# Decoder trunk on one core: input and first weights fetched in halves of the features, first four output tiles accumulated by halves of the contraction, products of ones ahead of the input

## The chip, the cores and the metric

The kernel runs on one core of a Trainium2 chip. The metric is the device time of one execution in microseconds (us), the median of several runs. The core has a matrix engine (TensorE, PE in the profile; its weight loads are PEld), a vector engine (VectorE, DVE), an activation engine (ScalarE, ACT), a general engine (GpSimd, POOL), and queues from which transfers between main memory and the on-chip memory are issued (SyncE's is SPq, ScalarE's is ACTq). Products accumulate in PSUM tiles, which TensorE writes and VectorE or ScalarE read.

## The reference, cut to what matters

Two layers, each a SwiGLU feed-forward half-step, a token-mixing sub-layer, and a second feed-forward half-step, over 16 learned tokens and 256 input tokens of 1024 features. The change touches the entry and the first half-step:

```
h = jnp.concatenate([meta, x], axis=1)          # 16 + 256 tokens, 1024 features
for l in range(DEPTH):                          # DEPTH = 2
    h = h + 0.5 * swiglu(rms_norm(h, ffn1_norm[l]), ffn1_w_gu[l], ffn1_w_down[l])
    ...                                         # token mixing, second half-step
return rms_norm(h, final_norm)[:, N_META:]

def swiglu(x, w_gu, w_down):
    gate, up = jnp.split(x @ w_gu, 2, axis=-1)  # each 2816 columns
    return (jax.nn.silu(gate) * up) @ w_down
```

## The kernel before

All activations lie feature-major: eight tiles `h[k]` of 128 features by 272 tokens (`L`). Every wide product is made three times, from parts that add up to the exact operand: weight high part times activation high part, weight high times activation low, weight low times activation high (`mm3`, lines 163 to 165). For that, each piece of weights (128 partitions by 1024 values) is rounded by ScalarE into a high part `wh` (line 144), and VectorE subtracts to get the low part `wl` (line 145); both have four buffers. The raw weights come in units of 1 MB (8 contraction steps by 256 columns) into `raw`, which has three buffers. The input rows `xr` also lie in one of these three.

At the start, x is loaded as two transfers of 128 tokens by 1024 features (lines 194 and 198), the learned tokens `mr` as two small ones (line 197), the small vectors `rows` as one (line 193, on ScalarE's queue). The first two weight units (gate and up of the first 256 columns) come as four transfers of 512 KB, one for each piece of 128 columns and all eight contraction steps (line 135); later units as one transfer each (line 132). For each `k` in 0 to 7, TensorE transposes 16 + 128 + 128 tokens into one PSUM tile (lines 916 to 918); `norm.split` scales by the gain and splits (ScalarE line 249, VectorE line 250); the tile is copied to `h[k]` (lines 923 and 925). Then `norm.square` squares each `h[k]` on ScalarE and adds it to `acc` on VectorE (lines 259 to 263). One product of ones with `acc` (line 273, in `rstd`) sums the squares over the features, and a chain on VectorE and ScalarE (lines 275 to 289) makes the token factor, which `finish` (lines 313 to 320) applies to finished gate and up tiles.

`ffn_up` takes two pairs of tiles (gate in a PSUM tile of tag `mm`, up in one of tag `aux`, four buffers of each tag) per step `f2`. For `f2 == 0` it takes the gate tiles first (pieces 0 and 1), then the up tiles (pieces 2 and 3): four output tiles by eight contraction steps by three products, 96 products. `piece()` prepares weights two pieces ahead.

The order of instructions on each engine is not the order of the program text alone. The Tile framework puts every engine's instructions in an order before the run, by priority and by the times that it computes, and an instruction that is ready early may be put ahead of others; `tc.issue_after(i)` forces instructions of the same engine behind `i` (`early` does that for the first two pieces). On the chip each engine then runs its list in order. `consts` loads the tables `cst` and makes the lower bounds of the forget gates; the program calls it at `f2 == 1`.

Of the kernel before, what the change touches and what calls it, by code (L numbers as in the profile page):

```python
# [52 lines left out]
def trunk(ctx: ExitStack, tc: tile.TileContext, a: dict):  # L53
# [13 lines left out]
    V, S, E, GP = nc.vector, nc.scalar, nc.tensor, nc.gpsimd  # L67

# [8 lines left out]

# [1 line left out]
    units, plan, ready, early = [], [], [], {}  # L79
    AHEAD = 2  # L80
# [44 lines left out]
    raws = {}  # L125

    def prepare(u, k0, kn, c0, cn):
        src, kt, cols, per, cuts = units[u]
        if u not in raws:
            raws[u] = T([P, 2048], F32, "raw", 3)[:, :kt * cols].rearrange("p (k c) -> p k c", k=kt)  # L130
            if u > 1:
                nc.sync.dma_start(out=raws[u], in_=src)
        rw = raws[u][:, k0:k0 + kn, c0:c0 + cn]
        if u < 2:
            nc.sync.dma_start(out=rw, in_=src[:, k0:k0 + kn, c0:c0 + cn])
        w2 = [T([P, 1024], F32R, t, 4)[:, :kn * cn].rearrange("p (k c) -> p k c", k=kn) for t in ("wh", "wl")]
# [6 lines left out]
        for x, hw, lw in views or [(rw, *w2)]:  # L143
            S.copy(out=hw, in_=x)  # L144
            V.tensor_tensor(out=lw, in0=x, in1=hw.bitcast(F32), op=ALU.subtract)  # L145
        return [tuple(w[:, k] for w in w2) for k in range(kn)]

    used = [0]

    # the next piece, as a list over its contraction steps  # L150
    def piece():
        used[0] += 1
        while len(ready) < min(used[0] + AHEAD, len(plan)):
            with ExitStack() as st:
                for i in early.pop(len(ready), ()):
                    st.enter_context(tc.issue_after(i.ins))
                ready.append(prepare(*plan[len(ready)]))
        r, ready[used[0] - 1] = ready[used[0] - 1], None
        return r
# [10 lines left out]

# [6 lines left out]
    parts, o = [], 0  # L177
    for n in (L, L, P, H, 32, NBLK * 32, P):
        parts.append(cst[:, o:o + n])
        o += n  # L180
    cos_t, sin_t, causal, bdmask, eye32, lv, rowsel = parts
    lvmask = lv.bitcast(I32).rearrange("p (n c) -> p n c", c=32)
# [6 lines left out]

# [11 lines left out]
    ps = PS("aux")  # L201
    E.transpose(out=ps[:, 0:76], in_=rows, identity=ident[0:76, 0:76])
    V.tensor_copy(out=cols, in_=ps[:, 0:76])
    F1, MX, F2, FN, QN, KVN, HGN, LB = 0, 16, 32, 48, 56, 62, 66, 68
# [3 lines left out]

    # lower bounds of the forget gates, by a softmax over the layers
    lbt = T([P, 8, G], F32, "lbt")  # L210
# [17 lines left out]
    qns = T([P, 6], F32, "qns")  # L228
    V.tensor_scalar(out=qns, in0=cols[:, QN:QN + 6], scalar1=DQK ** -0.5, scalar2=None, op0=ALU.mult)

    def lbc(l, g):
        return lbt[:, 4 + l, g:g + 1], lbt[:, 6 + l, g:g + 1]

# [1 line left out]
    class Norm:  # L235
# [10 lines left out]
        def split(self, k, src):  # L246
# [5 lines left out]
            self.parts[k] = (xh, xl)  # L252
            return i, j

        def square(self, k):
# [24 lines left out]

    # in steps, so that other work can stand between them
    def rsqrt(out, m, c):
# [13 lines left out]

    # two or more output tiles; the last contraction step of all of them comes last
    def mm_group(items, n):
# [5 lines left out]

# [1 line left out]
    def ffn_up(norm, c):  # L306
# [15 lines left out]
        def item(ps):  # L322
            w = piece()
            return ps[:, c], lambda k: w[k], lambda k: norm.x(k, c)

        for f2 in range(NF // 2):
            pairs = [(PS("mm"), PS("aux")) for j in range(2)]
            for j in range(2):
                mm_group([item(pairs[i][j]) for i in range(2)] if f2 == 0 else [item(ps) for ps in pairs[j]], KD)
                if f2 or j:  # L330
# [6 lines left out]
            if f2 == 1 and start:  # L337
                start.pop()()
        return acts
# [14 lines left out]

    # the last one, token-major, with the norm of the output
    def ffn_out(norm, c):
# [40 lines left out]

# [1 line left out]
    def mix(l, norm, nxt):  # L399
# [30 lines left out]

        # latent queries, latent keys and values (each with its norm), the shared rotary key
        def latents():
# [42 lines left out]
        def heads():  # L475
            kpe = st["kpe"]
            # queries
            wq = piece() + piece() + piece()
# [23 lines left out]
            yield  # L502
            # keys and values
            wkv = piece() + piece()
# [38 lines left out]

        # recurrence inputs
        lo = NM if last else 0
# [65 lines left out]

        # attention
        oa = []
# [81 lines left out]

        # recurrence, by halving
        am = T([P, 256], F32, "am", 1)
# [3 lines left out]
        def halving(gr):  # L701
# [3 lines left out]

            # products inside blocks of 32 tokens
            def blocks(li):
# [22 lines left out]

            # products between the halves of blocks of 2 b tokens
            def halves(b):
# [16 lines left out]
            for li, b in enumerate(LEVELS):  # L749
# [77 lines left out]

        # the wide products are dealt out among the steps of the two mixers
        def chain(*gens):
# [11 lines left out]

        # a branch's projection, times its gate
        mg = []
# [64 lines left out]

# [1 line left out]
    ca = slice(0, L)  # L910
    cs = slice(NM, L)
    norm = Norm(F1, ca)
    for k in range(KD):
        ps = PS("mm" if k < 4 else "aux")
        ks = slice(k * P, (k + 1) * P)
        E.transpose(out=ps[:, 0:NM], in_=mr[k // 4][0:NM, k % 4 * P:(k % 4 + 1) * P], identity=ident[0:NM, 0:NM])
        E.transpose(out=ps[:, 16:144], in_=xr[:, 0, ks], identity=ident)
        E.transpose(out=ps[:, 144:272], in_=xr[:, 1, ks], identity=ident)
        after = norm.split(k, ps[:, ca])
        if k in (1, 3):  # L920
            early[len(early)] = after
        if k % 2:
            S.copy(out=h[k], in_=ps[:, ca])
        else:
            V.tensor_copy(out=h[k], in_=ps[:, ca])
# [66 lines left out]
```

## Time and profile before

| | |
|---|---|
| device time, three runs | 1232.86, 1233.23, 1233.68 us; median 1233.23 |
| span of the profiled execution, first to last instruction | 1232.4 us |
| so outside the span, against the median | about 0.8 us |
| TensorE busy | 1216.2 us, 99% of the span |
| VectorE busy, ScalarE busy, GpSimd busy | 870.1, 643.7, 8.6 us |
| read from main memory | 200.89 MB, 164 GB/s over the span |

The profile is of one execution. Its page gives the busy time of each engine and the chain of work that ended last: followed back from the last instruction, at each step to what released it, or to the instruction before it on its engine. The trace behind it can be asked for a stretch of time. Times within the trace are microseconds from the start of the span. Matmuls are pipelined: the duration of one in a row overlaps the next, so that the distance between the starts of two, or the chain's entry, is what one costs.

### The profile page before, as it was taken

The numbers are of one execution on the slowest core, as the hardware profiler recorded it, in microseconds if no ns is written. First come the engines' busy times: TensorE is split into PE (matmuls) and PEld (weight loads), VectorE is DVE, ScalarE is ACT, GpSimd is POOL, SyncE is SP. The second block draws the span as 40 slices with busy tenths as digits, with TensorE's granted clock in tenths as the row PEclk, the third lists the DMA queues.
The fourth block names the chain that finished last, engine by engine and source line by source line (L and its number), as shares of the span: only waits on it lengthen the run. The fifth ranks groups of instructions, "written<-read, shape, count | busy, mean of one in ns | idle before, by whom it ended". The sixth has DMA issues, their size and how long they took to land.

```text
span 1232.4 us, 24345 instructions
## 1 busy us (share of the span) xinstructions
PE 1216.2 (99%) x10210; PEld 1175.0 (95%) x10210; DVE 870.1 (71%) x1585; ACT 643.7 (52%) x1073; POOL 8.6 (1%) x28
## 2 busy tenths in 40 slices
PE   7999999999999999999999999999999999999997
PEld 6999999999988999999999999999998899999986
DVE  5877755787866877776558776558869586977743
ACT  5544444566774644444445444445776655545442
POOL 0000000000000000000000000000000000000000
PEclk9999999999999999999999999999999999999999
DMA  7645555545332545646555546555454345555651
GB/s 225 204 149 196 177 179 178 173 142 158 122 134 86 189 141 168 201 148 211 163 165 174 183 160 197 187 156 173 140 168 138 120 138 172 191 172 186 206 188 52
DMA packets 188781, 203.50 MB, mean 165 GB/s; under 512 B 3348, under 2 KB 176480, under 8 KB 188672
## 3 DMA queue, kind: packets, MB, share of 16 engines
q1 hardware_dynamic: 188272, 201.36, 50.4%
q8 instruction: 80, 1.31, 0.4%
q10 hardware_dynamic: 400, 0.60, 0.1%
q14 instruction: 29, 0.24, 0.1%
HBM read 200.89 MB, written 1.05 MB: 164 GB/s over the span
## 4 chain that ended last, share of the span: by engine, by line
PE 96%; ACT 2%; DVE 1%; DMA 1%; issue 0%; SPq 0%; POOLq 0%; POOL 0%
PE pmm L163 21%; PE pmm L164 21%; PE pmm L165 21%; PE paux L164 7%; PE paux L165 7%; PE paux L163 7%; PE pmm L373 2%; PE pmm L374 2%; PE pmm L375 2%; PE paux L643 1%; PE paux L714 1%; PE paux L688 1%; DMA raw<-x 1%; ACT wh L144 0%; ACT act L501 0%; PE paux L800 0%
## 5 line engine op out<-in xcount | busy, mean ns | idle before, releaser
L144 ACT CAST wh<-raw 128x1024 fp32r<-128x1024 f32 (+3 forms) x398 | 398.4, 1006 | 388.7 <-PE pmm L164 263.0
L145 DVE TENSOR_TENSOR wl<-raw,wh 128x1024 fp32r<-128x1024 f32 (+3 forms) x398 | 464.4, 1170 | 172.5 <-ACT wh L144 170.7
L163 PE MATMUL pmm<-x,wh 128*128 128x272 f32 (+1 forms) x1312 | 381.1, 291 | 0.7 <-ACT act L513 0.7
L165 PE MATMUL pmm<-x,wl 128*128 128x272 f32 (+1 forms) x1312 | 375.8, 287 | 0.0
L164 PE MATMUL pmm<-x,wh 128*128 128x272 f32 (+1 forms) x1312 | 375.6, 286 | 0.0
L163 PEld LDWEIGHTS pmm<-x,wh 128*128 128x128 f32 x1312 | 246.8, 188 | 3.0 <-ACT act L513 1.0
L164 PEld LDWEIGHTS pmm<-x,wh 128*128 128x128 f32 x1312 | 247.0, 188 | 0.9
L165 PEld LDWEIGHTS pmm<-x,wl 128*128 128x128 f32 x1312 | 246.4, 188 | 0.2
L163 PE MATMUL pmm<-act,wh 128*128 128x272 f32 (+1 forms) x836 | 239.8, 287 | 0.0
L164 PE MATMUL pmm<-act,wh 128*128 128x272 f32 (+1 forms) x836 | 239.1, 286 | 0.0
L165 PE MATMUL pmm<-act,wl 128*128 128x272 f32 (+1 forms) x836 | 238.9, 287 | 0.0
L163 PE MATMUL paux<-x,wh 128*128 128x272 f32 (+1 forms) x704 | 201.1, 286 | 0.0
L164 PE MATMUL paux<-x,wh 128*128 128x272 f32 (+1 forms) x704 | 201.1, 286 | 0.0
L165 PE MATMUL paux<-x,wl 128*128 128x272 f32 (+1 forms) x704 | 201.1, 286 | 0.0
L163 PEld LDWEIGHTS pmm<-act,wh 128*128 128x128 f32 x836 | 157.3, 188 | 1.0 <-issue 0.8
L164 PEld LDWEIGHTS pmm<-act,wh 128*128 128x128 f32 x836 | 157.5, 188 | 0.4 <-issue 0.4
L165 PEld LDWEIGHTS pmm<-act,wl 128*128 128x128 f32 x836 | 157.0, 188 | 0.5 <-issue 0.3
L163 PEld LDWEIGHTS paux<-x,wh 128*128 128x128 f32 x704 | 132.8, 189 | 0.0
L164 PEld LDWEIGHTS paux<-x,wh 128*128 128x128 f32 x704 | 132.6, 188 | 0.0
L165 PEld LDWEIGHTS paux<-x,wl 128*128 128x128 f32 x704 | 132.5, 188 | 0.0
L168 ACT CAST act<-tmp 128x272 fp32r<-128x272 f32 (+1 forms) x88 | 36.5, 415 | 124.4 <-DVE tmp L317 124.4
L313 DVE TENSOR_TENSOR tmp<-pmm,rstd 128x272 f32<-128x272 f32 (+1 forms) x88 | 38.3, 435 | 50.9 <-PE pmm L165 50.6
(239 smaller groups left out, 1058.9 us busy)
## 6 DMA issues: line engine op xcount, KB each, us to landing
raw<-ffn_w_gu SPq DMA_DIRECT2D x86, 1024.0 KB, 5.3
raw<-w_in SPq DMA_DIRECT2D x36, 1024.0 KB, 5.2
raw<-ffn_w_down SPq DMA_DIRECT2D x34, 1024.0 KB, 5.2
raw<-ffn_w_down SPq DMA_DIRECT2D x12, 768.0 KB, 4.9
raw<-w_out SPq DMA_DIRECT2D x8, 1024.0 KB, 5.4
raw<-w_proj_attn SPq DMA_DIRECT2D x4, 1024.0 KB, 5.0
raw<-w_proj_rec SPq DMA_DIRECT2D x4, 1024.0 KB, 5.0
raw<-ffn_w_gu SPq DMA_DIRECT2D x4, 512.0 KB, 9.0
```

What stands on the lines that cost most here:

```text
L144: S.copy(out=hw, in_=x)
L145: V.tensor_tensor(out=lw, in0=x, in1=hw.bitcast(F32), op=ALU.subtract)
L163: E.matmul(ps, wh, xh, start=start, stop=False)
L164: E.matmul(ps, wh, xl, start=False, stop=False)
L165: E.matmul(ps, wl, xh, start=False, stop=stop)
L168: S.copy(out=hi_tile[:, c], in_=src)
L313: V.tensor_tensor(out=gt[:, c], in0=pg[:, c], in1=r[:, c], op=ALU.mult)
L373: E.matmul(pst[t], ah[:, ts_], wh, start=k == 0, stop=False)
L374: E.matmul(pst[t], al[:, ts_], wh, start=False, stop=False)
L375: E.matmul(pst[t], ah[:, ts_], wl, start=False, stop=k == NF - 1)
L643: E.matmul(ps[:, 0:n], qs[hd][0:DQK, TOK[i + 1][0]:TOK[i + 1][1]], kT[hd][0:DQK, 0:n], start=True, stop=True)
L688: E.matmul(ps[j * 64:j * 64 + 64, 16 + i * P:L], vt[1 + i][:, hd * 64:hd * 64 + 64], pts[hd][:, i * 256:256 + i * P], start=False, stop=i ...
```

## The change

The input x is fetched as four transfers instead of two: features 0 to 511 of both token blocks first, then, after the first half of the weights, features 512 to 1023. The first two weight units come as six transfers by contraction steps (steps 0 to 1, 2 to 3 of unit 0, 0 to 3 of unit 1; later 4 to 5, 6 to 7 of unit 0, 4 to 7 of unit 1), with all 256 columns. Both transfers of the learned tokens go to ScalarE's queue. The first four pieces are now 4 contraction steps by 256 columns, each cast in two halves (`first_piece`), between the splits. `first` goes through the four output tiles by contraction halves: gate and up for steps 0 to 3, then `second()` (transposes, splits and casts of the other half), then gate and up for steps 4 to 7. The squares and their sum move to GpSimd for this first norm (`square_aside`). Ten fp32 products of a 128 by 128 tile of ones stand ahead of everything on TensorE, and an `Exp` on ScalarE. Inside `hold()`, the instructions of VectorE, ScalarE and TensorE each keep the order of the program among themselves. Weights are prepared two pieces ahead only after `second()`.

```diff
+        def issue(*args, **kw):
+            if not Engine.held:
+                return f(*args, **kw)
+            if self.last is None:
+                self.last = f(*args, **kw)
+            else:
+                with tc.issue_after(self.last.ins):
+                    self.last = f(*args, **kw)
+            return self.last
...
-            plan.extend([pg[0], pu[0], pg[1], pu[1]] if f else pg + pu)
+            if f:
+                plan.extend([pg[0], pu[0], pg[1], pu[1]])
+            else:
+                plan.extend((p[0][0], k0, 4, 0, 256) for k0 in (0, 4) for p in (pg, pu))
...
+    def cast(x, hw, lw):
+        S.copy(out=hw, in_=x)
+        V.tensor_tensor(out=lw, in0=x, in1=hw.bitcast(F32), op=ALU.subtract)
...
+    def first_piece(u, k0):
+        w2 = parts(4, 256)
+        ready.append([tuple(w[:, k] for w in w2) for k in range(4)])
+        return [(raws[u][:, k0 + k:k0 + k + 2], *(w[:, k:k + 2] for w in w2)) for k in (0, 2)]
...
+    ones = T([P, P], F32, "ones")
+    V.memset(ones, 1.0)
+    busy = T([P, 1], F32, "busy")
+    S.activation(out=busy, in_=ones[:, 0:1], func=AF.Exp)
+    ps = PS("aux")
+    for _ in range(10):
+        E.matmul(ps[:, 0:P], ones, ones, start=True, stop=True)
     ident = T([P, P], F32, "ident")
     make_identity(nc, ident)
-    ones = T([P, P], F32, "ones")
-    GP.memset(ones, 1.0)
...
     nc.scalar.dma_start(out=rows, in_=a["vecs"])
-    nc.sync.dma_start(out=xr[:, 0, :], in_=a["x"][0, 0:P, :])
     mr = [T([P, 512], F32, "gv", 2) for _ in range(2)]
-    for i, q in enumerate((nc.scalar, nc.sync)):
-        q.dma_start(out=mr[i][0:NM], in_=a["meta_tokens"][:, i * 512:(i + 1) * 512])
-    nc.sync.dma_start(out=xr[:, 1, :], in_=a["x"][0, P:2 * P, :])
+    for i in range(2):
+        nc.scalar.dma_start(out=mr[i][0:NM], in_=a["meta_tokens"][:, i * 512:(i + 1) * 512])
+    for u in range(2):
+        raws[u] = raw_tile(u)
+    for i in range(2):
+        for t in range(2):
+            xs = slice(i * 512, i * 512 + 512)
+            nc.sync.dma_start(out=xr[:, t, xs], in_=a["x"][0, t * P:(t + 1) * P, xs])
+        for u in range(2):
+            for ks in (slice(4 * i, 4 * i + 4),) if u else (slice(4 * i, 4 * i + 2), slice(4 * i + 2, 4 * i + 4)):
+                nc.sync.dma_start(out=raws[u][:, ks], in_=units[u][0][:, ks])
...
+        def square_aside(self, k):
+            c = self.c
+            hk = h[k][:, c]
+            sq = tmp() if self.n else self.acc
+            GP.tensor_tensor(out=sq[:, c], in0=hk, in1=hk, op=ALU.mult)
+            if self.n:
+                GP.tensor_tensor(out=self.acc[:, c], in0=self.acc[:, c], in1=sq[:, c], op=ALU.add)
+            self.n += 1
...
+        def first(pairs):
+            for k0 in (0, 4):
+                for j in range(2):
+                    w = piece()
+                    for k1 in (0, 2):
+                        todo = [(pairs[i][j][:, c], w[k][0][:, i * P:(i + 1) * P], w[k][1][:, i * P:(i + 1) * P],
+                                 *norm.x(k0 + k, c), k0 + k) for k in (k1, k1 + 1) for i in range(2)]
+                        for ps, wh, wl, xh, xl, k in todo:
+                            E.matmul(ps, wh, xh, start=k == 0, stop=False)
+                            E.matmul(ps, wh, xl, start=False, stop=False)
+                        for ps, wh, wl, xh, xl, k in todo:
+                            E.matmul(ps, wl, xh, start=False, stop=k == KD - 1)
+                if k0 == 0 and len(start) > 1:
+                    start.pop(0)()
...
-    for k in range(KD):
-        ps = PS("mm" if k < 4 else "aux")
...
-    for k in range(KD):
-        norm.square(k)
+    def half(k0):
+        tiles = [PS("mm" if k in (4, 5) else "aux") for k in range(k0, k0 + 4)]
+        todo = first_piece(0, k0) + first_piece(1, k0)
+        for i, ps in enumerate(tiles):
+            k = k0 + i
+            ks = slice(k * P, (k + 1) * P)
+            E.transpose(out=ps[:, 0:NM], in_=mr[k // 4][0:NM, k % 4 * P:(k % 4 + 1) * P], identity=ident[0:NM, 0:NM])
+            E.transpose(out=ps[:, 16:144], in_=xr[:, 0, ks], identity=ident)
+            E.transpose(out=ps[:, 144:272], in_=xr[:, 1, ks], identity=ident)
+        for i, ps in enumerate(tiles):
+            norms[0].split(k0 + i, ps[:, ca])
+            if i != 1:
+                cast(*todo.pop(0))
+        for i, ps in enumerate(tiles):
+            (S.copy if i % 2 else V.tensor_copy)(out=h[k0 + i], in_=ps[:, ca])
+            norms[0].square_aside(k0 + i)
+        cast(*todo.pop(0))
+
+    def second():
+        with hold():
+            half(4)
+        ahead[0] = 2
 
     def consts():
         nc.sync.dma_start(out=cst, in_=a["c_all"])
-        lower_bounds()
-
-    start = [consts]
+        with hold():
+            lower_bounds()
+            V.tensor_scalar(out=qns, in0=cols[:, QN:QN + 6], scalar1=DQK ** -0.5, scalar2=None, op0=ALU.mult)
+
+    with hold():
+        half(0)
+    start = [second, consts]
```

## Rows read from the trace of the kernel before

**Rows 1.** The page: busy time by engine, and the chain that ended last.

```profile
PE 1216.2 (99%) x10210; PEld 1175.0 (95%) x10210; DVE 870.1 (71%) x1585; ACT 643.7 (52%) x1073; POOL 8.6 (1%) x28
...
PE 96%; ACT 2%; DVE 1%; DMA 1%; issue 0%; SPq 0%; POOLq 0%; POOL 0%
```

**Rows 2.** The chain from 0 to 60 us: start, us on the chain, what.

```profile
1.65 6.34 DMA raw<-x
8.04 0.47 PE pmm L918
...
14.35 0.23 PE pmm L163
...
17.75 0.17 PE pmm L165
...
27.92 0.46 PE paux L273 x2
```

**Rows 3.** Busy time of each engine in three stages, with the granted clock (PEclk).

```profile
8.04:14.35 6.31, 6.31 (x23) 3.84 (x24) 4.85 (x10) 5.55 (x13) 0.00 (x0) 1.00 1.10 299
14.35:17.55 3.20, 3.20 (x16) 3.20 (x16) 3.20 (x7) 3.20 (x7) 0.00 (x0) 1.00 0.67 227
...
20.00:27.92 7.92, 7.92 (x65) 7.92 (x64) 4.82 (x13) 2.79 (x4) 0.00 (x0) 1.00 0.65 209
```

**Rows 4.** Three transposes among products, later in the run, in order of time.

```profile
256.94 0.27 PE L586 MATMUL paux<-ident,tmp 128*128 128x128 f32 x1
...
257.15 0.27 PE L588 MATMUL paux<-ident,tmp 128*16 128x128 f32 x1
```

**Rows 5.** Four fp32 products of 128 columns (eight records), late, and the product after them.

```profile
1194.61 1.06 PE L377 MATMUL pmm<-ident,h 128*128 128x128 f32 x8
1195.42 0.48 PE L373 MATMUL pmm<-wh,act 128*128 128x512 f32 x1
```

**Rows 6.** The start in order of time.

```profile
6.42 0.18 PEld L916 LDWEIGHTS pmm<-ident,gv 16*128 16x128 f32 x1 [0.31 <-DMA gv<-meta_tokens]
...
6.71 0.15 DVE L214 TENSOR_TENSOR lbt<-cols 128x4 f32<-128x4 f32 x1
...
8.55 0.49 ACT L249 ACTIVATE x<-pmm,cols 128x272 fp32r<-128x272 f32 x1 [0.59 <-PE pmm L918]
```

**Rows 7.** Splits and the input's transfers, 0 to 30 us: ns min/median/max.

```profile
L250 DVE SCALAR_TENSOR_TENSOR x<-paux,cols,x x4: 489/492/500, 14.7 to 18.6; 128x272 fp32r<-128x272 f32 x4
...
DMA to landing us min/median/max: 5.3/5.8/6.3
```

**Rows 8.** Casts and transfers of the weight units, 0 to 70 us.

```profile
L132 SPq DMA_DIRECT2D raw<-ffn_w_gu x11: 367/368/443, 14.4 to 67.7; - x11
...
DMA to landing us min/median/max: 4.8/6.3/9.7
```

**Rows 9.** VectorE in order of time: operations of 272 columns, then a cast of 1024.

```profile
42.52 0.43 DVE L315 SCALAR_TENSOR_TENSOR tmp<-paux,rstd 128x272 f32<-128x272 f32 x1
42.87 0.43 DVE L313 TENSOR_TENSOR tmp<-pmm,rstd 128x272 f32<-128x272 f32 x1
...
44.62 1.22 DVE L145 TENSOR_TENSOR wl<-raw,wh 128x1024 fp32r<-128x1024 f32 x1
45.76 0.43 DVE L169 TENSOR_TENSOR act<-tmp,act 128x272 fp32r<-128x272 f32 x1
```

**Rows 10.** What the chip moved in two stretches of 1 us (3 to 4, 6 to 7).

```profile
DMA packets 150, 0.39 MB, mean 389 GB/s; under 512 B 22, under 2 KB 50, under 8 KB 150
...
DMA packets 536, 0.32 MB, mean 315 GB/s; under 512 B 4, under 2 KB 524, under 8 KB 536
```

**Rows 11.** GpSimd's groups, whole run: count, busy us, mean ns.

```profile
L756 POOL COPY at<-cb 32x128 f32<-32x128 f32 x16 | 5.2, 326 | 937.7 <-DVE cb L726 937.0
L186 POOL MEMSET at<- 128x768 f32 x2 | 1.4, 737 | 0.0
```

**Rows 12.** VectorE in order of time: the first use of the token factor.

```profile
34.54 0.44 DVE L313 TENSOR_TENSOR tmp<-pmm,rstd 128x272 f32<-128x272 f32 x1
```

More of the change, by code (lines that the diff above doesn't have):

```diff
@@ L1 @@
-from contextlib import ExitStack
+from contextlib import ExitStack, contextmanager
 import numpy as np
@@ L65, in PS, with __init__, __getattr__, hold @@
         return pp.tile([P, 512], F32, name=f"p{tag}_{counter[0]}", tag=tag, bufs=4)
-    V, S, E, GP = nc.vector, nc.scalar, nc.tensor, nc.gpsimd
+    class Engine:
+        held = False
+        def __init__(self, e):
+            self.e, self.last = e, None
+        def __getattr__(self, name):
+            f = getattr(self.e, name)
+            def issue(*args, **kw):
[7 more added lines that the diff above has]
+                return self.last
+            return issue
+    @contextmanager
+    def hold():
+        Engine.held = True
+        yield
+        Engine.held = False
+    V, S, E, GP = Engine(nc.vector), Engine(nc.scalar), Engine(nc.tensor), nc.gpsimd
     def xt():
@@ L76, in tmp @@
         return T(list(shape), dt, tag, bufs)
-    units, plan, ready, early = [], [], [], {}
-    AHEAD = 2
+    units, plan, ready = [], [], []
+    ahead = [0]
     def add(src, kt, cols, per=None, cuts=None, by_k=False):
@@ L125, in trunk, with raw_tile @@
     raws = {}
+    def raw_tile(u):
+        kt, cols = units[u][1:3]
+        return T([P, 2048], F32, "raw", 3)[:, :kt * cols].rearrange("p (k c) -> p k c", k=kt)
     def prepare(u, k0, kn, c0, cn):
@@ L129, in prepare @@
         if u not in raws:
-            raws[u] = T([P, 2048], F32, "raw", 3)[:, :kt * cols].rearrange("p (k c) -> p k c", k=kt)
-            if u > 1:
-                nc.sync.dma_start(out=raws[u], in_=src)
+            raws[u] = raw_tile(u)
+            nc.sync.dma_start(out=raws[u], in_=src)
         rw = raws[u][:, k0:k0 + kn, c0:c0 + cn]
-        if u < 2:
-            nc.sync.dma_start(out=rw, in_=src[:, k0:k0 + kn, c0:c0 + cn])
-        w2 = [T([P, 1024], F32R, t, 4)[:, :kn * cn].rearrange("p (k c) -> p k c", k=kn) for t in ("wh", "wl")]
+        w2 = parts(kn, cn)
         views, off = [], 0
@@ L142, in prepare, with parts @@
             off += n
-        for x, hw, lw in views or [(rw, *w2)]:
-            S.copy(out=hw, in_=x)
-            V.tensor_tensor(out=lw, in0=x, in1=hw.bitcast(F32), op=ALU.subtract)
+        for v in views or [(rw, *w2)]:
+            cast(*v)
         return [tuple(w[:, k] for w in w2) for k in range(kn)]
+    def parts(kn, cn):
+        return [T([P, 1024], F32R, t, 4)[:, :kn * cn].rearrange("p (k c) -> p k c", k=kn) for t in ("wh", "wl")]
+    def cast(x, hw, lw):
[5 more added lines that the diff above has]
+        return [(raws[u][:, k0 + k:k0 + k + 2], *(w[:, k:k + 2] for w in w2)) for k in (0, 2)]
     used = [0]
@@ L152, in piece @@
         used[0] += 1
[L153 to L157, printed above, removed]
+        while len(ready) < min(used[0] + ahead[0], len(plan)):
+            ready.append(prepare(*plan[len(ready)]))
         r, ready[used[0] - 1] = ready[used[0] - 1], None
@@ L169, in split @@
         V.tensor_tensor(out=lo_tile[:, c], in0=src, in1=hi_tile[:, c].bitcast(F32), op=ALU.subtract)
+    ones = T([P, P], F32, "ones")
[5 more added lines that the diff above has]
+        E.matmul(ps[:, 0:P], ones, ones, start=True, stop=True)
     ident = T([P, P], F32, "ident")
     make_identity(nc, ident)
-    ones = T([P, P], F32, "ones")
-    GP.memset(ones, 1.0)
     cst = T([P, 2 * L + P + H + 32 + NBLK * 32 + P], F32, "cst")
-    parts, o = [], 0
+    tables, o = [], 0
     for n in (L, L, P, H, 32, NBLK * 32, P):
-        parts.append(cst[:, o:o + n])
+        tables.append(cst[:, o:o + n])
         o += n
-    cos_t, sin_t, causal, bdmask, eye32, lv, rowsel = parts
+    cos_t, sin_t, causal, bdmask, eye32, lv, rowsel = tables
     lvmask = lv.bitcast(I32).rearrange("p (n c) -> p n c", c=32)
@@ L193, in trunk @@
     nc.scalar.dma_start(out=rows, in_=a["vecs"])
-    nc.sync.dma_start(out=xr[:, 0, :], in_=a["x"][0, 0:P, :])
     mr = [T([P, 512], F32, "gv", 2) for _ in range(2)]
-    for i, q in enumerate((nc.scalar, nc.sync)):
-        q.dma_start(out=mr[i][0:NM], in_=a["meta_tokens"][:, i * 512:(i + 1) * 512])
-    nc.sync.dma_start(out=xr[:, 1, :], in_=a["x"][0, P:2 * P, :])
+    for i in range(2):
+        nc.scalar.dma_start(out=mr[i][0:NM], in_=a["meta_tokens"][:, i * 512:(i + 1) * 512])
+    for u in range(2):
+        raws[u] = raw_tile(u)
+    for i in range(2):
[5 more added lines that the diff above has]
+                nc.sync.dma_start(out=raws[u][:, ks], in_=units[u][0][:, ks])
     cols = T([P, 76], F32, "cols")
-    ps = PS("aux")
-    E.transpose(out=ps[:, 0:76], in_=rows, identity=ident[0:76, 0:76])
-    V.tensor_copy(out=cols, in_=ps[:, 0:76])
+    with hold():
+        ps = PS("aux")
+        E.transpose(out=ps[:, 0:76], in_=rows, identity=ident[0:76, 0:76])
+        V.tensor_copy(out=cols, in_=ps[:, 0:76])
     F1, MX, F2, FN, QN, KVN, HGN, LB = 0, 16, 32, 48, 56, 62, 66, 68
@@ L324, in item @@
             return ps[:, c], lambda k: w[k], lambda k: norm.x(k, c)
+        def first(pairs):
[12 more added lines that the diff above has]
+                    start.pop(0)()
         for f2 in range(NF // 2):
             pairs = [(PS("mm"), PS("aux")) for j in range(2)]
+            if f2 == 0:
+                first(pairs)
             for j in range(2):
-                mm_group([item(pairs[i][j]) for i in range(2)] if f2 == 0 else [item(ps) for ps in pairs[j]], KD)
+                if f2:
+                    mm_group([item(ps) for ps in pairs[j]], KD)
                 if f2 or j:
@@ L337, in ffn_up @@
             if f2 == 1 and start:
-                start.pop()()
+                start.pop(0)()
         return acts
@@ L912, in trunk @@
     norm = Norm(F1, ca)
-    for k in range(KD):
-        ps = PS("mm" if k < 4 else "aux")
[L915 to L925, printed above, removed]
-    for k in range(KD):
-        norm.square(k)
+    norms = [norm]
+    def half(k0):
[19 more added lines that the diff above has]
+        ahead[0] = 2
     def consts():
         nc.sync.dma_start(out=cst, in_=a["c_all"])
-        lower_bounds()
-    start = [consts]
+        with hold():
+            lower_bounds()
+            V.tensor_scalar(out=qns, in0=cols[:, QN:QN + 6], scalar1=DQK ** -0.5, scalar2=None, op0=ALU.mult)
+    with hold():
+        half(0)
+    start = [second, consts]
     for l in range(DEPTH):
```

1 line of the change is left out of this document (removed).

## The prediction

> **What bounds the kernel now.** I read the page first, then the chain of waits at the start, then the stages of the start one by one. The page shows TensorE busy for 99% of the span and holding 96% of the chain [rows 1]: the other engines matter only where they make TensorE wait. The change alters only the entry, so the question is how early TensorE has the first 96 products behind it (call that moment T96). After it, the same products follow in both kernels.
>
> The chain shows the entry [rows 2]. The second half of the tokens lands at 8.0, and TensorE transposes for 6.3 us. From 14.35 it makes products 0.227 us apart, from 17.75 on 0.125 apart (81 products in 10.2 us, up to the ones-product of line 273 at 27.92). T96 is 27.9. In these stages it is never idle [rows 3]; the way to an earlier T96 is an earlier start or the same work at a higher clock. The granted clock reads 1.00 throughout, but 272 columns in 0.227 us are 1.2 GHz, and the later spacing is near 272 columns at 2.4 GHz. So the first 15 products ran at the lower level and cost 1.5 us too much; 6.3 us of transposes had not raised it, 3.2 us of products did. A set of three transposes costs 0.83 us there (23 of the 24 transposes in the 6.31 us of the stage [rows 3]), but three transposes amid products, later, take about 0.32 us (0.21 between first and third start, and one more spacing) [rows 4].
>
> **The change, step by step.**
>
> *Products of ones.* Four fp32 products of 128 columns take 0.81 us at the higher clock [rows 5], so ten take 2.0, or 4.1 at the lower. They can start once VectorE has filled the tile, about 1 us, and end near 5, before the learned tokens land at 6.42 [rows 6]: cost nothing; that wait is the cover. If the input came before 5, they would delay it. They may raise the clock; no row shows whether it stays up until the products. Bounds: low throughout the first half, or high from the first transpose. I take high, since products, not transposes, raised it, and price low as a rival. The `Exp` brings a table load ahead, in the same idle time.
>
> *Input by halves.* The first two transfers now carry 512 KB, as the first did, and that one landed 5.3 us after its issue at 0.74, so at 6.0 [rows 7]. The learned tokens are still needed, at 6.4. Transposes thus start at 6.4 in place of the 8.0 for the full set, 1.6 us earlier, and the ScalarE split at 7.0 in place of 8.55 [rows 6]. The queue now issues ten transfers for these in place of seven, at about 0.4 us each some 4 us. Behind the first 0.6 MB the chip moves about 0.3 MB per us [rows 10]: the first weights (0.26 MB) land near 7, the second half of x, at a cumulative 2.2 MB, 10.7 to 11.4. Both are estimates from these rates and the 2 us between the last byte and the landing that the first x transfer shows. The second learned-token transfer moves behind two others on ScalarE's queue and is not needed before the second half.
>
> *VectorE becomes the pace of a half.* A split lasts 0.49 us [rows 7], a 272-column operation starts 0.35 after the one before, a 1024-column cast 1.14 before the next [rows 9], so a half cast of 512 about 0.60 and a split about 0.42. One half is 4 splits, 4 half casts and 2 copies: 1.7 + 2.4 + 0.7 = 4.8 us, against 48 x 0.125 = 6.0 us of products. ScalarE has as many operations, each somewhat shorter, and runs one ahead. From the split at 7.0, VectorE starts 7.5. Step 0's products can start at 8.0 but step 1's low part comes at 9.0, step 3's at 10.4; gate products end at 11.4. The up tiles sit in `aux` buffers that held the transposes, freed by the copies at 11.4. The last cast is done at 12.3. So 48 products end at 14.4: 6.0 of work and 0.4 of gaps.
>
> *Second half.* In program order its transposes follow. Four sets are 1.3 us; then TensorE waits for splits: step 4's low part is there at 15.7, step 5's at 16.7, step 7's at 18.1, casts to 20.0; products end at 22.1. If the list has the transposes earlier, in the gaps, T96 is 21.1. Line 214 ran at 6.71 though called at `f2 == 1` [rows 6], so instructions do move. Moved too early, they would hold TensorE until x lands at 11: then about 11.3 + 12.0 + 0.9 = 24.2. I take 22.1.
>
> *Weights after it.* The third unit takes the input's buffer, so its transfer starts when the last transpose ends: 14.4 now (first issue of line 132 [rows 8]), 13.5 us before T96. Then it starts at 15.7, 6.4 us before T96. A unit lands 4.8 us or more after issue (6.3 median, with others in flight) [rows 8]: 20.5 to 22, and the casts (ScalarE about 1, VectorE 1.1) end at 22.6 to 24.1. The third product of the unit needs the low part. So TensorE loses 0.5 to 2.0 us here; I take 1.3. The fourth unit, in the buffer of the first, is released by a cast at 17.7 and needed 2.6 us after the third; it lands about as late, no further loss. The order on the queue is unchanged otherwise.
>
> *Squares on GpSimd.* This takes seven additions and eight squares off VectorE and ScalarE, which is in the sum above. GpSimd gets a chain of 15 two-input operations on 272 columns. No row shows one. Bounds: 0.43 us, VectorE's price [rows 9], and 1.4 us, twice the copy of 128 columns (0.326) scaled to 272 [rows 11]. I take 0.8. The second half's eight begin near 19.1, when `h[4]` is copied, and end 25.5, while the product of line 273 stands after T96 in the program. Where the list puts it among the next products it costs nothing; directly after T96 up to 2 us. I take 0.3. The token factor is first used at 34.54 [rows 12], and the next pair needs its PSUM tiles only after another 96 products (12.0 us after 28.4, at 40.4), so a delay of 3 us behind T96 is covered by 5 us.
>
> On the last step the Trainium skill (GPSIMD Engine Reference, sections 1 and 3.1) speaks against the move: two-input elementwise work costs about 2.6 cycles an element at 1.2 GHz, for 272 columns an estimated 0.6 us by that page, and GpSimd shares its memory interface with VectorE when that reads two on-chip inputs, as each cast does. By its price alone the chain ends near 24; with sharing it goes toward my upper bound. No row here shows either.
>
> **The sum.** T96 from 27.9 to 22.1 is -5.8; +1.3 for the weights, +0.3 for the ones-product, +0.2 for whatever a changed order costs later: -4.0 us. The span goes from 1232.4 to 1228.4, and with the 0.8 us around it, the median from 1233.2 to 1229.2.
>
> **The rivals.**
>
> *Transposes in the gaps.* T96 21.1 and the third unit lands in time: -6.6, about 1226.6. For it: instructions moved before; against: x may be late on the chip.
>
> *Low clock, or TensorE held by x.* With 14 or so products at 0.227, +1.4, and sets at 0.83 in both halves, +2 or less beyond the gaps: T96 24 to 24.5; the blocked variant gives 24.2. The third unit is then nearly in time: -2.5, about 1230.7. For it: 2 or 3 us between ones and products. The Trainium skill (TensorE: Matmul & The Clock Gate, parts 1 and 4) makes the lower level the default after idleness and says that transposes don't count as activity; rows of before agree on the second, and by it this case would come out.
>
> *Weights eat the gain.* If the third and the fourth unit each land 6.3 us or more after issue and one cast queues behind the other, 4 us go: -1.5, about 1231.7. For it: the three buffers; against: 4.8 us is the least seen [rows 8], and the queue is empty by then.
>
> *GpSimd ends late (slower).* If an operation takes 1.4 us, the 15, from 11.4, end at 32.4; with line 273 directly after T96, everything behind it waits in TensorE's list: +4.5, about 1237.7. It decides from 1.1 us per operation (no gain, 27.9) and turns measurably slower at 1.27. Against: the list may put that product later.
>
> **Chances.** Forecast 0.50, transposes in the gaps 0.13, low clock or held 0.17 (it straddles the limit), weights 0.11, GpSimd 0.09. The limit of what can be told here is 0.2%, 2.5 us. Faster: 0.50 + 0.13 + half of 0.17, about 0.71; same: the other half and the weights, 0.20; slower 0.09. The likeliest case alone, by its unknown costs (weights 0.5 to 2.0, T96 by 1 us), spans 1227.7 to 1230.8. The range from 1226.6 to 1232.4 takes in that, the gaps, the low clock and the weights, and leaves out GpSimd's case and the tails.
>
> **What would show it.** In the profile after: the first set of transposes at 6.4 and about 0.3 us a set; products 0.125 apart from 8; VectorE without a gap from 7.5 to 12; the line of the ones-product with `acc` near 22 to 24; a wait of TensorE for `wh` or `wl` of the third unit of 1 to 2 us; GpSimd's 15 operations at 0.6 to 1.0 us. The prediction is wrong if TensorE stands at that ones-product for GpSimd, if the products before 15 us lie 0.227 apart, or if the order of later stages brings waits that were not there.

## The result and the profile after

The changed kernel takes 1237.11 us (median of 8 runs, 1236.85 to 1237.76), the kernel before 1233.53 (8 runs, 1232.86 to 1234.33): ratio 1.0029, 95% interval 1.0018 to 1.0039. It is 3.6 us slower, and 1229.2 was forecast. The forecast case did not come; the rival that ends slower did, in part.

In the trace of the changed kernel nearly every instruction carries line 79, because all calls of three engines pass through the new `issue`; line 81 is the first held instruction of an engine, line 84 the later ones. So this profile is read by tiles. The chain from 0 to 60 us (start, us, what) answers to [rows 2]:

```profile
1.05 4.33 PE paux L79 x20
...
5.47 2.19 PE paux L84 x12
7.66 0.63 PE pmm L79 x5
...
10.93 3.00 PE paux L79 x24
13.93 0.54 PE pmm L84 x3
...
19.07 1.69 POOL tmp L313 x2
20.76 0.73 POOL nacc L315
...
22.81 1.58 POOL tmp L313
24.39 0.72 POOL nacc L315
25.11 0.07 issue
25.18 0.77 POOL nacc L315
25.95 0.04 issue
25.99 1.28 PE paux L79 x2
27.27 5.29 PE pmm L79 x24
32.55 0.25 PE paux L79 x2
...
33.05 3.00 PE paux L79 x24
```

Up to 19 us the chain is TensorE and VectorE, as forecast, with two entries of ScalarE. Then it is GpSimd, up to the product of ones with `nacc` at 25.99. After that, 24 products take 5.29 us, and 24 others, from 33.05, take 3.00. In order of time the end of the first 96 products, GpSimd's last operations and the cast on VectorE beside them look like this (shortened):

```profile
21.53 0.66 PE L79 MATMUL paux<-x,wl 128*128 128x272 f32 x4
22.05 0.75 POOL L315 TENSOR_TENSOR nacc<-nacc,tmp 128x272 f32<-128x272 f32 x1
...
22.48 1.40 DVE L79 TENSOR_TENSOR wl<-raw,wh 128x1024 fp32r<-128x1024 f32 x1 [0.90 <-ACT wh L79]
22.77 1.62 POOL L313 TENSOR_TENSOR tmp<-h 128x272 f32<-128x272 f32 x1
...
24.35 1.59 POOL L315 TENSOR_TENSOR nacc<-nacc,tmp 128x272 f32<-128x272 f32 x2
25.99 0.50 PEld L79 LDWEIGHTS paux<-nacc,ones 128*128 128x128 f32 x2 [4.02 <-POOL nacc L315]
25.99 1.28 PE L79 MATMUL paux<-nacc,ones 128*128 128x272 f32 x2 [3.80 <-POOL nacc L315]
```

The 96 products end at 21.53 + 0.66 = 22.2. The ones-product (line 273 in the kernel before) is the next in TensorE's list, and TensorE stands 3.80 us for `nacc`. Busy time by stage (PE, PEld, DVE, ACT, POOL, then the granted clock, DMA share, GB/s), to be read beside [rows 3]:

```profile
5.50:25.30 19.80, 16.68 (x120) 14.79 (x120) 13.93 (x26) 9.88 (x22) 11.71 (x15) 1.00 0.83 272
25.50:32.10 6.60, 6.11 (x25) 5.88 (x26) 3.88 (x11) 4.26 (x5) 0.44 (x1) 0.50 0.19 63
32.30:41.50 9.20, 9.20 (x75) 9.20 (x75) 7.85 (x14) 4.78 (x8) 0.00 (x0) 1.00 0.68 221
```

After the idle stretch the granted clock stood at 0.50, the 1.2 GHz level, and TensorE worked at it from 26.0 to 32.1: 6.1 us at half the rate cost 3.05 more. Wait and fall together are 6.85 us, more than the whole lead over the kernel before.

### The profile page after: what moved, and what is told of

It is laid out like the page before. It is cut to its first block, busy times and chain, and to the rows that moved or that the text cites. A ratio compares the mean times of both kernels' runs of the same rounds, so it can differ in the third digit from the quotient of the medians.

```text
span 1235.0 us, 24403 instructions
## 1 busy us (share of the span) xinstructions
PE 1221.1 (99%) x10230; PEld 1180.6 (96%) x10230; DVE 870.7 (71%) x1583; ACT 642.3 (52%) x1070; POOL 20.9 (2%) x42
## 4 chain that ended last, share of the span: by engine, by line
PE 97%; ACT 1%; POOL 1%; DVE 1%; issue 0%; POOLq 0%
PE pmm L79 70%; PE paux L79 27%; ACT act L79 1%; POOL tmp L313 0%; ACT wh L79 0%; POOL nacc L315 0%; PE paux L84 0%; DVE tmp L79 0%; DVE wl L84 0%; DVE wl L79 0%; DVE x L84 0%; DVE gk L79 0%; ACT gq L79 0%; ACT pm L79 0%; POOLq L1084 0%
## 5 line engine op out<-in xcount | busy, mean ns | idle before, releaser
L79 PE MATMUL pmm<-x,wh 128*128 128x272 f32 (+1 forms) x2624 | 497.0, 289 | 0.7 <-ACT act L79 0.7
L79 PEld LDWEIGHTS pmm<-x,wh 128*128 128x128 f32 x2624 | 406.7, 188 | 4.4 <-ACT act L79 1.0
L79 PE MATMUL pmm<-act,wh 128*128 128x272 f32 (+1 forms) x1672 | 311.7, 287 | 0.0
L79 PE MATMUL paux<-x,wh 128*128 128x272 f32 (+1 forms) x1408 | 262.1, 286 | 0.0
L79 PEld LDWEIGHTS pmm<-act,wh 128*128 128x128 f32 x1672 | 260.6, 188 | 1.3 <-issue 1.2
L79 PEld LDWEIGHTS paux<-x,wh 128*128 128x128 f32 x1408 | 216.4, 188 | 0.0
L79 DVE TENSOR_TENSOR tmp<-tmp,tmp 128x272 f32<-128x272 f32 (+1 forms) x180 | 77.0, 430 | 1.7 <-ACT tmp L79 1.1
L79 DVE TENSOR_TENSOR act<-tmp,act 128x272 fp32r<-128x272 f32 (+1 forms) x88 | 38.3, 436 | 33.0 <-ACT act L79 33.0
L79 PE MATMUL pmm<-wh,act 128*128 128x512 f32 x192 | 60.8, 396 | 0.0
L79 ACT ACTIVATE tmp<-tmp 128x272 f32<-128x272 f32 (+1 forms) x110 | 46.5, 423 | 10.7 <-DVE tmp L79 10.7
```

The lines of the kernel that those rows point to most:

```text
L79: return f(*args, **kw)
```

## The experiments

Times of experiments are medians beside runs of the kernel before on the same chip; ratios are to those. The changed kernel's 1237.11 is from the result. The edits are shortened where lines stand as `...`.

**e1: the ones-product later.** The product with the sum of squares stands 26 products further back.

```diff
+        late = norm is norms[0]
...
-                    if factor is not None and next(factor, pend) is pend:
-                        factor = None
+                    for _ in range(0 if late and f2 == 0 else 2 if late and f2 == 1 and j else 1):
+                        if factor is not None and next(factor, pend) is pend:
+                            factor = None
```

> The changed kernel with one thing moved: the product of ones with the sum of squares stands 26 products later on TensorE. Theory (GpSimd ends late, TensorE waits 3.8 us at that product, and the lower clock that follows the wait costs another 3): no wait, no fall of the clock; the first 96 products end at 22.2 as in the changed kernel, a wait of about 1 us for the third weight unit appears, and the time is 5 to 6 us below the changed kernel's, 1231 to 1232. Rival (most of the loss lies elsewhere, in a slower later run or outside the span): within 2 us of the changed kernel.

Measured: 1233.80, before 1233.41, ratio 1.0005 (0.9996 to 1.0014); 3.3 us below the changed kernel, where 5 to 6 was expected. No wait for GpSimd and no fall of the clock. The 96 products end at 22.8 here, not 22.2: the first set of transposes still went at the lower level. And the next wait is there, larger than expected. The chain of this run:

```profile
16.67 5.15 DMA raw<-ffn_w_gu
...
21.89 1.06 ACT wh L79
...
22.98 1.53 DVE wl L79
...
24.55 2.64 PE pmm L79 x19
```

The third weight unit starts at 16.67, when the input's buffer is free, lands at 21.8, and its low part is ready at 24.5. After the 96 products TensorE does two more, and the third starts at 24.55, about 1.7 us later than without a wait. A second wait of 0.7 us follows at 36.8, for a cast of later weights. So the theory holds for the first wait, and about 1 us was too little for what comes behind it: 2.4.

**e2: squares back.** The squares and their sum on ScalarE and VectorE, behind the last cast of each half.

```diff
-            norms[0].square_aside(k0 + i)
         cast(*todo.pop(0))
+        for i in range(4):
+            norms[0].square(k0 + i)
```

> The changed kernel with the squares and their sum on ScalarE and VectorE again, behind the last cast of each half. Theory: the sum is ready near 21.8, before the 96 products end, so no wait and no fall of the clock; 5 to 6 us below the changed kernel, 1231 to 1232. If VectorE is the bound of the second half, the four additions there delay the third unit's low part by up to 1.4 us: then 1232 to 1233. Rival (GpSimd is only a symptom): within 2 us of the changed kernel.

Measured: 1232.39, ratio 0.9991 (0.9982 to 1.0000); 4.7 us below the changed kernel, the case between 1232 and 1233. Its reason was another than expected: the low part of the third unit waited for the high part, not for the additions. The ones-product ran at 23.5 without a wait. The chain names the loss that remains, the fourth unit, whose transfer began at 18.25 while the third's, issued at 16.67, was still running:

```profile
18.25 7.55 DMA raw<-ffn_w_gu
...
25.83 1.06 ACT wh L79
...
26.91 1.24 DVE wl L79
...
28.19 2.64 PE paux L79 x19
```

**e3: the wait filled.** The changed kernel with 17 products of ones between the 96 products and the ones-product, so that TensorE is busy while GpSimd works.

```diff
...
+                if norm is norms[0]:
+                    ps = PS("aux")
+                    with tc.issue_after(norm.mm.ins):
+                        for _ in range(17):
+                            norm.mm = E.matmul(ps[:, 0:P], ones, ones, start=True, stop=True)
```

> The changed kernel with 17 more fp32 products of ones (3.6 us at the higher clock) between the first 96 products and the product of ones with the sum of squares; TensorE is busy there instead of idle, and the end of GpSimd's chain is as before. Theory that the fall of the clock is half of the loss: the wait is filled, the clock stays up, and the time is about 3 us below the changed kernel's, 1234. Rival (the clock's fall costs nothing, only the wait does): the same as the changed kernel, 1237.

Measured: 1234.70, before 1233.41, ratio 1.0011 (1.0002 to 1.0021); 2.4 us below the changed kernel, though 17 useless products were added and the ones-product ran no earlier:

```profile
19.49 6.67 PE paux L79 x57
...
26.18 0.73 PE paux L79 x2
26.90 2.63 PE pmm L79 x21
```

21 products now take 2.63 us there, 0.125 each, and the granted clock is 1.00 from 26 to 33 us. The fall of the clock is a price of its own beside the wait, 2.4 us by the medians.

**e4: no products ahead.** The ten products of ones left out.

```diff
-    for _ in range(10):
+    for _ in range(0):
```

> The changed kernel without the ten products of ones ahead of the input. Theory (they raise the clock before the input): sets of transposes at 0.83 us in place of 0.53, the first products 0.227 apart, the first 96 products end 1.5 to 2.5 us later, near 24; GpSimd's chain ends about 1 later, near 27, so the wait there is shorter and the clock may stay up: 1234 to 1238. If the ones cost something later in the run or outside the span (rival), the drift of about 1.5 us over the run and the extra time outside the span go away too: 1232 to 1234.

Measured: 1238.64, ratio 1.0042 (1.0025 to 1.0059); 1.5 us above the changed kernel and above the expected 1234 to 1238. The first twelve transposes take 3.40 us in place of 2.19, and the ones-product comes 1.95 us later. The wait for GpSimd is about the same, 3.9 us: that it would be shorter was wrong, since GpSimd's chain moves with the start. The clock fell here too (mean 0.76 from 26 to 33 us), but products lay at the lower spacing for only 3.1 us behind the wait, to 31.0, where the changed kernel's profile has 6.1.

```profile
PE paux L79 <- POOL nacc L315: 3.9, 1, 3.9
```

**e5 and e6: placement, first theory.** From about 40 us on, the same products in nearly the same order ran slightly slower in the changed kernel, evenly over the run, some 1.5 us in all: over 10230 products that is about 0.15 ns each, not the 0.5 ns of the expectation. The one-column tile `busy` moves every later tile by 32 bytes; one run makes it 64, another adds 32 to the kernel before.

```diff
-    busy = T([P, 1], F32, "busy")
+    busy = T([P, 16], F32, "busy")
...
```

> The changed kernel with the one-column tile of the early Exp made 16 columns wide, so that everything behind it in the on-chip memory lies 64 bytes further than without that tile, not 32; nothing else. In the traces so far, products late in the changed kernel lie some 0.5 ns further apart than the same products before, 1.5 us over the run. Theory A (where the operands lie in memory sets that): the drift goes, 1.2 to 1.8 us below the changed kernel, 1235.3 to 1235.9. Rival (the drift is of the profiled execution or of something else in the change): 1237.

```diff
     ones = T([P, P], F32, "ones")
+    pad = T([P, 1], F32, "pad")
+    GP.memset(pad, 0.0)
```

> The kernel before with one added tile of 32 bytes per partition behind the tile of ones (set to zero by GpSimd), so that every later tile lies 32 bytes further; nothing else. Theory A (placement): slower by 1 to 2 us than before, with the drift of the changed kernel. Rival: no change.

Measured: 1237.06 (ratio 1.0031, 1.0020 to 1.0043) and 1233.17 (0.9998, 0.9990 to 1.0007). Neither moved. That theory fell.

**e7: input aside.** Squares back, the 64-byte tile, and the input in four tiles that are free until the mixers.

```diff
-    xr = T([P, 2048], F32, "raw", 3).rearrange("p (t d) -> p t d", t=2)
+    xq = [[T([P, 512], F32, n, 2) for n in ("gq", "gk")] for _ in range(2)]
...
```

> Squares on ScalarE and VectorE as in e2_squares_back, the 64-byte tile of e5_aligned, and the input rows in four tiles that are free until the mixers, so that the third weight unit need not wait for the input's buffer. Theory (what is left of the gain in e2 goes to the third and fourth units, whose transfers start at 16.7 and 18.3 and land at 22.0 and 25.8, and to the placement): first 96 products end at 22.2, no wait for the third unit, at most 1 us for the fourth; 4 to 5.5 us below before, 1228 to 1229.5. Rival (without the placement): 1229.5 to 1231. If the earlier transfers delay the first weights: 1230 or more.

Measured: 1230.17, before 1233.50, ratio 0.9974 (0.9965 to 0.9983). Faster than both kernels, though not the expected 1228 to 1229.5 but the rival's 1229.5 to 1231, in which the placement does not change. The third and fourth units no longer make TensorE wait, and between 1 and 200 us one wait is left, that for the tile of ones at the start:

```profile
PE paux L79 <- DVE ones L79: 1.1, 1, 1.1
```

**e8: squares on GpSimd alone.** The kernel before with `square_aside` for the first norm.

```diff
...
     for k in range(KD):
-        norm.square(k)
+        norm.square_aside(k)
```

> The kernel before with this one part of the change: the first norm's squares and their sum on GpSimd. There the first 96 products end at 27.8 and the last copy to h near 19.5, so a chain of 15 operations at 0.6 to 1.6 us ends at 22 to 27. Theory (GpSimd costs only because the first 96 products end early): no wait of TensorE, within 0.5 us of before, and 0.3 us more outside the span as in the runs with squares on GpSimd. Rival (GpSimd's operations slow VectorE's and so the start): 1 to 3 us slower.

Measured: 1233.31, ratio 1.0001 (0.9992 to 1.0009). In this kernel GpSimd's chain ends about when TensorE comes to the product, here at 26.26, just ahead of it (out of the chain and GpSimd's timeline):

```profile
25.49 0.77 POOL L261 TENSOR_TENSOR nacc<-nacc,tmp 128x272 f32<-128x272 f32 x1
...
26.33 0.71 PE paux L282 x2
```

So the part costs nothing that shows, with no room to spare. Outside the span its runs have 2.05 us, the runs of before 1.78.

**e9: products ahead alone.** The kernel before with the ten products of ones.

```diff
+    ones = T([P, P], F32, "ones")
+    V.memset(ones, 1.0)
+    ps = PS("aux")
+    for _ in range(10):
+        E.matmul(ps[:, 0:P], ones, ones, start=True, stop=True)
...
```

> The kernel before with this one part of the change: ten fp32 products of ones on TensorE ahead of the input (the tile of ones filled by VectorE). Theory (they raise the clock before the input): a set of transposes 0.53 us in place of 0.83, no products 0.227 apart, so the first 96 products end some 3.5 us earlier if VectorE and ScalarE follow; with their splits and casts between, 2 to 3.5 us below before, 1230 to 1231.5. Rival (they add nothing without the halves, since VectorE is then the pace): within 1 us of before.

Measured: 1232.55, ratio 0.9995 (0.9986 to 1.0004): the rival's case, no difference that is clear of the noise. In the profiled execution the ten products ran, and yet the transposes and the first products went at the lower level, as in [rows 2]:

```profile
8.28 0.21 PE pmm L919
8.49 0.41 PE pmm L920
8.90 0.21 PE pmm L921
...
14.34 0.23 PE pmm L164
14.56 0.23 PE pmm L165
```

It is not the common execution: it took 1233.88, with a mean granted clock of 0.999, and eight of the eleven have 0.995 or 0.996. What the products did to the clock there no trace shows.

**e10, e11 and e12: placement, second theory.** In the changed kernel the first pieces of weights are made before the first splits. So the program asks for the tiles `wh` and `wl` first, and by that order they should lie below `x` and `tmp` in the on-chip memory; before, above. The addresses themselves no trace shows. Three runs touch one tile of a pair early (one column set to zero) to choose the order: the faster kernel placed as before, the kernel before placed as after, and the changed kernel placed as before.

```diff
+    for t in (xt(), tmp()):
+        GP.memset(t[:, 0:1].bitcast(F32), 0.0)
```

> The kernel of e7_squares_back_input_aside with one thing changed: an x tile and a tmp tile are touched (one column set to zero by GpSimd) before the weights' tiles, so that x and tmp lie below wh and wl in the on-chip memory, as in the kernel before; in the changed kernel they lie above. Theory B (the order of these tiles in memory sets the 1.4 us of drift over the run): 1.2 to 1.6 us below e7, about 1228.8. Rival (the drift has another cause): 1230.2.

```diff
+    for t in ("wh", "wl"):
+        GP.memset(T([P, 1024], F32R, t, 4)[:, 0:1].bitcast(F32), 0.0)
```

> The kernel before with one thing changed: a wh and a wl tile are touched (one column set to zero by GpSimd) before the first x tile, so that wh and wl lie below x and tmp, as in the changed kernel. Theory B: 1.2 to 1.6 us slower than before, about 1234.9. Rival: no change, 1233.5.

```diff
+    for t in (xt(), tmp()):
+        V.memset(t[:, 0:1].bitcast(F32), 0.0)
```

> The changed kernel with one thing changed: an x tile and a tmp tile are touched (one column set to zero by VectorE) before the weights' tiles, so that x and tmp lie below wh and wl, as in the kernel before. Theory B (this order is a part of the loss of its own, beside the wait for GpSimd and the fall of the clock): 0.7 to 1.5 us below the changed kernel, 1235.6 to 1236.4, with the wait of 3.8 us and the fall of the clock still there, so still 2 to 3 us slower than before. Rival (the placement acts only where the start is without a wait): 1237.1.

Measured: 1229.41 (0.9967, 0.9954 to 0.9979), 1234.70 (1.0011, 1.0002 to 1.0020) and 1235.97 (1.0021, 1.0012 to 1.0030): 0.8 us better than e7, 1.3 worse than before, 1.1 better than the changed kernel. All three moved the way of the theory; e11 and e12 by what it said, e10 by less than its 1.2 to 1.6. The first is the fastest kernel of the study. The count of products in the same 440 us, with TensorE busy throughout, shows it (columns as above). Before, changed, before placed as after, changed placed as before:

```profile
420.00:860.00 440.00, 440.00 (x3519) 439.20 (x3518) 303.22 (x472) 209.68 (x302) 0.00 (x0) 1.00 0.54 175
```

```profile
420.00:860.00 440.00, 440.00 (x3513) 439.19 (x3512) 303.40 (x472) 210.31 (x301) 0.00 (x0) 1.00 0.55 175
```

```profile
420.00:860.00 440.00, 440.00 (x3513) 439.21 (x3512) 302.99 (x472) 209.35 (x300) 0.00 (x0) 1.00 0.55 174
```

```profile
420.00:860.00 440.00, 440.00 (x3517) 439.19 (x3516) 304.05 (x473) 210.37 (x302) 0.00 (x0) 1.00 0.55 175
```

The time between the first and the last of 32 operations that all kernels have shows it without counting. The same four, in the same order:

```profile
L648 ACT ACTIVATE pm<-paux,sm x32: 380/434/496, 311.9 to 959.3; 128x144 f32<-128x144 f32 x16, 128x272 f32<-128x272 f32 x16
L79 ACT ACTIVATE pm<-paux,sm x32: 381/434/494, 313.6 to 962.0; 128x144 f32<-128x144 f32 x16, 128x272 f32<-128x272 f32 x16
L648 ACT ACTIVATE pm<-paux,sm x32: 380/432/491, 311.1 to 959.5; 128x144 f32<-128x144 f32 x16, 128x272 f32<-128x272 f32 x16
L79 ACT ACTIVATE pm<-paux,sm x32: 381/436/496, 313.2 to 961.1; 128x144 f32<-128x144 f32 x16, 128x272 f32<-128x272 f32 x16
```

These are 647.4, 648.4, 648.4 and 647.9 us. Every profile with the order of before (e6, e8, e9) has 647.3 or 647.4, every one with that of the changed kernel (e1 to e5, e7) 648.4 or 648.5, and e10 has 647.9. The shares of busy time, the granted clock and the transfers are the same, so the views of waits and shares do not show this loss. A touch also takes one buffer of its tile out of turn, which no run separates from the order; but the changed kernel loses the same 1.0 us without a touch.

## Why the prediction was wrong

**The start was right.** The 96 products were forecast to end at 22.1 and ended at 22.2. That they agree to 0.1 is in part luck: in the profiles of e1, e2 and e5, with the same start, the products end at 22.8. And on the way some terms were off and cancelled: transposes began at 5.47, not 6.4, because the learned tokens landed earlier, so that the products of ones ended last; a set took 0.53 us, not 0.32, though the clock was up (the 0.32 was read from three transposes amid products [rows 4]); VectorE's first half ran from 6.6 to 11.9 (forecast 7.5 to 12.3); the second half's transposes stood behind all products of the first and began at 13.86 (forecast 14.4).

**The step that failed is the ones-product.** GpSimd's chain was forecast to end at 25.5 and ended at 25.95. An addition took 0.76 us; a square took 0.64 alone and 1.62 beside a cast on VectorE, more than the 1.4 that was set as the upper bound:

```profile
L313 POOL TENSOR_TENSOR tmp<-h x7: 641/1083/1617, 9.6 to 22.8; 128x272 f32<-128x272 f32 x7
L315 POOL TENSOR_TENSOR nacc<-nacc,tmp x7: 752/759/770, 12.4 to 25.2; 128x272 f32<-128x272 f32 x7
```

But "directly after T96 up to 2 us. I take 0.3" fails twice. By the prediction's own numbers TensorE would stand 25.5 - 22.1 = 3.4 us there; 2 is what is left of that beside the 1.3 already counted for the weights, which the text does not say. And it was put down at 0.3 because the list might have the product later, for which no row spoke. In [rows 2] it also stands directly behind the 96 products. It stood there again, and the wait was 3.80; this is the first of the signs that the prediction itself named for being wrong. The sum had 1.3 + 0.3 = 1.6 us behind the 96 products; 6.85 came.

**What no step priced was the fall of the clock behind that wait**, 3.05 us by the stage's rows, 2.4 by the filled wait (e3). It is not the same in every execution: in the profiles of e4, e5 and e12, with the same wait, the products lay at the lower spacing for a little over 3 us, not 6.1. The rival that ends slower names the right mechanism, a chain on GpSimd that ends after the 96 products, but puts the limit at 1.1 us per operation, since it counts the wait alone. With 0.86 us on average in the second half (6.9 us for eight) the lead was already gone. So the case that the range leaves out came at a lower price per operation than the prediction thought it needed.

**Two smaller terms were missed.** For whatever a changed order costs later 0.2 us was set; the placement of the tiles costs 1.1 (e12) to 1.5, through the order in which the program first asks for them. And the runs with squares on GpSimd have 2.05 to 2.2 us outside the span, those without 1.8; that adds 0.3 to 0.4, for which there was no term.

**The base was off.** "0.8 us around" the span set the median of the runs against a span of another execution. The runs of before have 1.8 us outside, and spans from 1230.5 to 1232.9, so the profiled 1232.4 lies high among them. The entry varies: the second half of the tokens was there at 8.04 in the profile of before, at 7.36 in that of e6 and at 6.94 in that of e8, whose entries are like it. In the profile of e8 the products reach the higher level at 15.7, not 17.75:

```profile
15.06 0.23 PE pmm L165
15.29 0.42 PE pmm L163 x2
15.72 0.13 PE pmm L164
```

There the ones-product comes at 26.33. So the lead of the changed kernel at the end of its 96 products is 4.1 to 5.7 us, by which profile of the entry one takes; 5.8 was forecast.

**The account behind the 96 products closes better.** From there to the end of the span the profiles of before, e6, e8 and e9 have 1204.5 to 1204.7 us, those of e7 and e11, with the other placement and no such wait, 1206.0, and the changed kernel 1212.8. That is 8.3 more than before: 3.80 for the wait, 3.05 for the clock, 1.5 for the placement. With 0.35 outside the span and the lead taken off, this is 2.9 to 4.5 us slower, and 3.6 was measured. Where in its range the lead of the usual execution lies, no trace says.

**The weights** were forecast to cost 1.3 us behind the 96 products. In the changed kernel that is hidden in the longer wait; with it gone, it is 2.4 us in e1, and taking the input out of the weights' buffers removes it: e7 is 2.2 us below e2. **The products ahead** are followed by transposes at the higher level in most profiled executions, not in all (e9, e10), and without the rest they bring nothing that is clear of the noise (e9: 0.9 us by the medians); within the change they are worth 1.5 us (e4).

The Trainium skill (GPSIMD Engine Reference, sections 1 and 3.1) gave 2.6 cycles an element, by which such an operation was an estimated 0.6 us, and warned of the interface shared with VectorE. The trace is in line with both: 0.64 us for a square and 0.76 for an addition alone, up to 1.62 for a square beside a cast.

## What to carry to other kernels

When work that was hidden behind a stage is moved to a slower engine and the same change shortens that stage, compare the new end of the one with the new end of the other, and take the consumer to be where the list of its engine had it before. Price a wait of TensorE with the clock that it may lose, not by its own length alone: here 3.8 us of wait brought 3.05 more. And where a change alters the order in which tiles are first asked for, count products per stretch late in the run: the same work can go 0.15% slower with no wait to be seen.

## What was not expected of the hardware

- After 3.8 us without work TensorE ran the next 6.1 us at 0.50 of its clock in the changed kernel's profile; after a like wait it ran a little over 3 us at that level in those of e4, e5 and e12.
- When the program asks for `wh` and `wl` before `x` and `tmp`, the same work takes 0.15% longer (648.4 against 647.4 us; 3513 against 3519 products in 440 us); 32 or 64 bytes of shift do nothing (e5, e6). Why the order matters stays open.
- Ten fp32 products of ones before the input are followed by transposes at 0.53 us a set in the changed kernel, but at 0.83 in the profiled execution of e9, and in that of e10, where twelve take 3.33 us. When they raise the clock stays open.
- Fifteen two-input operations on GpSimd go with 0.3 to 0.4 us more outside the span, in all seven kernels that have them (the changed one, e1, e3, e4, e5, e8, e12); what happens there no profile shows.
